# Gated DeltaNet on one core: another order of the input products in three stretches, and later starts for the eight recurrences

## The chip, the cores and the metric

The kernel runs on one core of a Trainium2 chip. The metric is the device time of one execution in microseconds (us); lower is better. The engines are named as the profile names them: PE is TensorE's matmul (PEld its weight load), DVE is VectorE, ACT is ScalarE, POOL is GpSimd, and SP is SyncE, which issues nearly all DMAs. Each engine works through its own instructions strictly in the order of the program and waits on semaphores for the others.

## The reference, cut to what matters

The whole program is one inference step of a two-layer trunk: a gated DeltaNet layer, then an RWKV-7 layer, over 1,104 token rows (64 sample rows, 16 meta tokens, 1,024 prompt rows). The change touches the gated DeltaNet layer alone. Its core, cut from the reference:

```
proj = xn @ w_in                                  # q, k, v and the gate z for all heads
qkv, new_buf = causal_conv(qkv, conv_buf, conv_w) # 4 taps along the tokens, then SiLU
L = jnp.where(strict, jnp.einsum('nbhik,nbhjk->nbhij', kb, k) * decay, 0.0)
A = L + jnp.eye(chunk, dtype=L.dtype)
sol = lax.linalg.triangular_solve(A, rhs, left_side=True, lower=True, unit_diagonal=True)
u, wk = sol[..., :DV], sol[..., DV:]
def step(S, inp):                                 # once a chunk, in order
    v_new = u_c - jnp.einsum('bhck,bhkv->bhcv', w_c, S)
    o = jnp.einsum('bhck,bhkv->bhcv', qd_c, S) + jnp.einsum('bhij,bhjv->bhiv', a_c, v_new)
    S = S * jnp.exp(gl_c)[..., None, None] + jnp.einsum('bhck,bhcv->bhkv', kd_c, v_new)
o = rmsnorm(o, gn_w) * jax.nn.silu(z.reshape(B, T, GDN_V_HEADS, GDN_HEAD_V))
```

There are 16 value heads and 8 query/key heads, so a key head serves a pair of value heads. For each pair: project q, k, two v's and two z's; convolve q, k and v; invert a unit lower triangular matrix for each block of tokens; run the recurrence over the blocks; normalise and gate.

## The kernel before

**Pairs, products, stretches, slots.** The layer is worked in eight pairs of value heads, j = 0 to 7. Each pair needs six products with the resident input: keys `k`, queries `q`, values `v` and `w`, gates `x` and `y`. A product has three token segments (384, 384 and 336 wide), a segment 24 matmuls, issued in two halves of 12. A half with whatever is hung behind it is a **slot**; a product is six slots. The products stand in eight stretches, one string of `ORDER` each: the first has four products (slots -24 to -1), the next six have six (36 slots each), the last has eight. In the stretch of pair j the gates `x`, `y` are those of pair j-1. Slot 0 is the start of the stretch of pair 1, slot 36 that of pair 2, and so on; the products end at slot 264.

**Events.** All other work of PE and ACT in this part is hung on slot numbers by `at(u, f)`: an event with u in [n, n+1) is issued behind the matmuls of slot n. For PE and ACT the order in the program is this order by hand. DVE, POOL and SP take their order from the scheduler of the framework, which merges what the events give.

**What a product hangs on DVE.** The conv of one segment of k, q, v or w is three multiply-adds on DVE (L526, writes `cvy`; the first tap is on ACT), then the SiLU (L532, one instruction, two in the first segment). A gate segment is one DVE instruction (L834, `zg`). A segment of values is then turned by three PE transposes (`f`) and scaled on DVE into `bv` (L825, method `gdn_value_rows`).

**The inverse.** For each pair, scores of the keys (L702 to L712) go through DRAM into the tile `invA`: 72 blocks of 32x32, inverted together on DVE by 31 steps of two instructions (L573 `invtmp`, L575 `invT`), released two or three at a time by the events `inv`. The event `spread` (time `sp`) issues the rest, copies the transpose (L743 `invA`), and sends the inverse through DRAM (`g_t`, `g_u`) into the tiles `T1n` and `TT`. The four `merges` then join the 32-blocks on PE: `y32` (writes `rY`, the first reader of `T1n`), `u32` (`rU`), `y64` and `u64`. They stand 6.5, 4.5, 3.5 and 1.5 slots ahead of the recurrence's start a.

**The recurrence.** It begins at slot a = `first[j]` (one call at a-1, then 26 calls, one a slot). A block of tokens takes three slots: k·S and q·S on PE, X on DVE (L883; L880 and L881 in block 0); TT·X on PE, w on ACT; the new state S (L905) and output o (L916) on DVE. The PE tiles of it are `rA`. The state of block n is read by PE one slot after it is asked for. Norms, gating (`mog` on PE, L1077 on DVE) and stores follow at fixed distances from a.

**What `first` sets.** In `front_events` the score decays, the inverse and others are placed by a0, the start of the recurrence before, as well as by the stretch's own base b; for pairs 3 to 7 the inverse starts at k + 9.3 with k = e + 4.7 and e = a0 - 3.4 as a rule, that is a0 + 10.6.

## Time and profile before

| | |
|---|---|
| Median of 3 runs | 2171.39 us (2170.72 to 2176.32) |
| The profiled execution: time, span | 2173.21 us, 2171.5 us |
| Granted TensorE clock, mean | 0.982 |
| PE busy | 2046.2 us, 94% |
| PEld busy | 1905.8 us, 88% |
| DVE busy | 1583.4 us, 73% |
| ACT busy | 1283.1 us, 59% |
| POOL busy | 834.9 us, 38% |

Slot -24 begins at 39.8 us of the span and the last product ends at 1014.6 us. The starts of the stretches are 105.07, 247.18, 376.52, 496.24, 615.36, 734.30, 853.10 and 972.54 us (slots 0, 36, ... 252). "Idle before" in a row of the timeline is the time that this engine did nothing just before it, with what ended it. A waiting engine holds up everything behind it on its own queue. PE busy includes the pipelined ends of matmuls, so a stretch with PE at 99% has no room that shows as idle.

### The profile page before, as it was taken

What the parts mean: (1) busy time and instruction counts of PE and PEld (TensorE: products, weight loads), DVE (VectorE), ACT (ScalarE), POOL (GpSimd) and SP (SyncE); (2) the same over time, 40 slices, a digit from 0 to 9 for tenths busy, and PEclk for the clock granted to TensorE, in tenths of its full rate; (3) what the DMA queues carried; (4) which work ended last, traced back from release to release, by engine and by line L of the source; (5) the groups of instructions that cost most, each with busy time, mean ns of one, the idle gap of its engine ahead of it and who ended that gap; (6) DMA issues with size and microseconds to landing.
All of it is one profiled execution on the core that took longest, in us unless ns stands there. A gap on an engine that the chain in (4) does not pass through costs nothing. (4 is left out here: it accounts for less than half of the span.)

```text
span 2171.5 us, 54811 instructions
## 1 busy us (share of the span) xinstructions
PE 2046.2 (94%) x20418; PEld 1905.8 (88%) x20418; DVE 1583.4 (73%) x4212; ACT 1283.1 (59%) x3750; POOL 834.9 (38%) x1136
## 2 busy tenths in 40 slices
PE   6969899999999999999999999889899999999997
PEld 5959899999999999998899999889798988888876
DVE  6968879698888979795334676757979557767755
ACT  4536565656565665656533365664747446677774
POOL 3523334334343333334231352344524254444444
PEclk9979999999999999999999999999999999999999
DMA  3424343424333333335345115655555486677754
GB/s 120 122 58 105 77 108 90 118 79 107 90 97 106 106 97 104 97 102 159 106 129 135 63 54 191 220 160 174 169 180 158 117 224 175 188 234 225 228 178 139
DMA packets 430724, 292.52 MB, mean 135 GB/s; under 512 B 147337, under 2 KB 413050, under 8 KB 430458
## 3 DMA queue, kind: packets, MB, share of 16 engines
q1 hardware_dynamic: 430458, 289.02, 46.2%
q8 instruction: 161, 2.64, 0.5%
q14 instruction: 105, 0.86, 0.1%
HBM read 197.55 MB, written 91.37 MB: 133 GB/s over the span
## 5 line engine op out<-in xcount | busy, mean ns | idle before, releaser
L91 POOL TENSOR_TENSOR wlo<-wraw,whi 128x512 fp32r<-128x512 f32 (+1 forms) x246 | 331.1, 1348 | 465.6 <-ACT whi L87 413.9
L77 PE MATMUL d<-xc,whi 128*128 128x384 f32 (+2 forms) x1006 | 279.5, 337 | 4.8 <-ACT whi L87 4.1
L526 DVE SCALAR_TENSOR_TENSOR cvy<-raw,cw,cvy 128x408 f32<-128x408 f32 (+2 forms) x288 | 199.0, 692 | 17.1 <-ACT cvy L63 15.7
L87 ACT CAST whi<-wraw 128x512 fp32r<-128x512 f32 (+1 forms) x246 | 149.8, 611 | 88.1 <-PE d L77 51.2
L77 PEld LDWEIGHTS d<-xc,whi 128*128 128x128 f32 (+1 forms) x1006 | 183.4, 189 | 7.8 <-ACT whi L87 4.8
L77 PE MATMUL d<-xc,wlo 128*128 128x384 f32 (+3 forms) x476 | 157.7, 340 | 2.7 <-POOL wlo L91 2.7
L77 PE MATMUL dz<-xc,whi 128*128 128x384 f32 (+1 forms) x480 | 153.9, 338 | 0.0
L77 PE MATMUL dv<-xc,whi 128*128 128x384 f32 (+1 forms) x480 | 152.4, 337 | 0.0
L77 PE MATMUL d<-xa,whi 128*128 128x384 f32 (+3 forms) x450 | 142.1, 340 | 4.5 <-ACT whi L87 1.7
L63 ACT ACTIVATE o<-rA,gcol 128x128 f32<-128x128 f32 x128 | 42.0, 366 | 116.9 <-DVE S L905 116.7
L573 DVE TENSOR_TENSOR invtmp<-invA,invT 72x31 f32<-72x31 f32 (+15 forms) x248 | 102.2, 412 | 3.2
L77 PE MATMUL dv<-xa,whi 128*128 128x384 f32 (+1 forms) x288 | 99.1, 344 | 0.0
L77 PE MATMUL dz<-xa,whi 128*128 128x384 f32 (+1 forms) x288 | 98.6, 342 | 0.0
L575 DVE TENSOR_TENSOR invT<-invT,invtmp 72x31 f32<-72x31 f32 (+15 forms) x248 | 95.0, 383 | 3.3
L77 PEld LDWEIGHTS d<-xc,wlo 128*128 128x128 f32 (+1 forms) x476 | 89.3, 189 | 6.8 <-POOL wlo L91 3.6
L77 PEld LDWEIGHTS dz<-xc,whi 128*128 128x128 f32 x480 | 89.4, 189 | 4.6 <-issue 4.5
L77 PEld LDWEIGHTS d<-xa,whi 128*128 128x128 f32 (+1 forms) x450 | 83.9, 189 | 8.2 <-issue 3.7
L77 PEld LDWEIGHTS dv<-xc,whi 128*128 128x128 f32 x480 | 89.2, 188 | 1.4 <-issue 1.4
L77 PE MATMUL d<-xa,wlo 128*128 128x384 f32 (+3 forms) x252 | 84.9, 337 | 1.4 <-POOL wlo L91 1.4
L77 PE MATMUL dk<-xc,whi 128*128 128x384 f32 (+1 forms) x240 | 79.3, 349 | 0.0
L77 PE MATMUL dq<-xc,whi 128*128 128x384 f32 (+1 forms) x240 | 77.0, 338 | 0.0
L1335 DVE SCALAR_TENSOR_TENSOR mixs<-xb,pcol,mixs 128x320 f32<-128x320 f32 (+2 forms) x96 | 68.6, 725 | 5.9 <-ACT mixs L63 5.6
(542 smaller groups left out, 6801.0 us busy)
## 6 DMA issues: line engine op xcount, KB each, us to landing
wraw<-in_gdn_w_in SPq DMA_DIRECT2D x96, 256.0 KB
wraw<-in_rwkv_w_rkvz SPq DMA_DIRECT2D x80, 256.0 KB
Sb<-in_state_gdn SPq DMA_DIRECT2D x64, 256.0 KB
sldcak<-cakd SPq DMA_DIRECT2D x24, 576.0 KB
wraw<-in_rwkv_w_o SPq DMA_DIRECT2D x42, 256.0 KB
E<-drow SPq DMA_DIRECT2D x24, 384.0 KB
attn<-drow SPq DMA_DIRECT2D x24, 384.0 KB
wraw<-in_gdn_w_out SPq DMA_DIRECT2D x36, 256.0 KB
```

What stands on the lines that cost most here:

```text
L63: return self.nc.scalar.activation(out, in_, func, bias=bias, scale=scale, **kw)
L77: self.nc.tensor.matmul(out, lhsT, rhs, start=start, stop=stop)
L87: nc.scalar.copy(hi, x)
L91: e.tensor_tensor(lo, x, hi.bitcast(F32), op=ALU.subtract)
L526: nc.vector.scalar_tensor_tensor(y[0][:, 0:wd], raw[:, k:k + wd], cw[k], y[0][:, 0:wd], op0=ALU.mult, op1=ALU.add)
L573: nc.vector.tensor_tensor(tmp, A[:, j, j + 1:32].unsqueeze(2).broadcast_to([nb, n, m]), Tv[:, j, 0:m].unsqueeze(1).broadcast_to([nb, n, m] ...
L575: nc.vector.tensor_tensor(Tv[:, j + 1:32, 0:m], Tv[:, j + 1:32, 0:m], tmp, op=ALU.subtract)
L1335: nc.vector.scalar_tensor_tensor(x[:, f:], xb[:, 8 + a + f:8 + b], mu, x[:, f:], op0=ALU.mult, op1=ALU.add)
```

## The change

Three things, all in where work stands; nothing is computed otherwise.

1. The second stretch (pair 1) goes from `kxyqvw` to `xkyvqw`: gate, keys, gate, values, queries, values. The third and fourth go to `kxyvqw`.
2. The recurrences start later. In slots: 9, 43, 78, 114, 150, 186, 222, 258 before; 14.5, 48.5, 83.5, 118.5, 153.5, 188.5, 224.5, 260.5 now. The gaps between them are 34, 35 and five times 36 before; 34, four times 35 and twice 36 now. Events placed by a or a0 move with them; products don't.
3. The sample states of pairs 3 to 7 are not loaded before a0 + 3.3, and their value rows not before a0 + 5.8 + 9s (two limits that held for earlier pairs only).

```diff
-ORDER = ("kqvw", "kxyqvw", "kxyqvw", "kxyqvw", "kxyqvw", "kxyqvw", "kxyqvw", "kxyqvwXY")
+ORDER = ("kqvw", "xkyvqw", "kxyvqw", "kxyvqw", "kxyqvw", "kxyqvw", "kxyqvw", "kxyqvwXY")
...
-        first = [9, 43] + [base[j + 1] + 6 for j in range(2, 8)]
+        first = [14.5, 48.5, 83.5, 118.5, 153.5] + [base[j + 1] + 8.5 for j in range(5, 8)]
...
-                inv, per, kk, ss, rd = [k + 9.3 + n for n in range(15)], 2, (b + 11.8, qb + 4.2), b + 13.2, (qb + 6.4, qb + 9.9)
+                inv, per, kk, ss, rd = [k + 9.3 + n for n in range(15)], 2, (b + 11.8, qb + 4.2), max(b + 13.2, a0 + 3.3), (qb + 6.4, qb + 9.9)
...
-                u = max(v + 5.4 + 2 * s, a0 + 9 * s + 5.8 + 0.2 * h if 0 < j < 3 else -99)
+                u = max(v + 5.4 + 2 * s, a0 + 9 * s + 5.8 + 0.2 * h if j else -99)
```

On DVE, in the second half of the inverse of pair 0, at the start of the second stretch (slots 0 to 6). Before:

```order
L573 TENSOR_TENSOR invtmp_1117<-invA_921,invT_923 72x255
L526 SCALAR_TENSOR_TENSOR cvy_1461<-raw_1400,cw_404,cvy_1461 128x408
L575 TENSOR_TENSOR invT_923<-invT_923,invtmp_1117 72x17x15
L532 SCALAR_TENSOR_TENSOR vt_1472<-raw_1315,cvy_1381 128x336
L526 SCALAR_TENSOR_TENSOR cvy_1461<-raw_1400,cw_404,cvy_1461 128x408
L573 TENSOR_TENSOR invtmp_1146<-invA_921,invT_923 72x256
L526 SCALAR_TENSOR_TENSOR cvy_1461<-raw_1400,cw_404,cvy_1461 128x408
L809 TENSOR_SCALAR qeps_1003<-qeps_1003 128x9
L575 TENSOR_TENSOR invT_923<-invT_923,invtmp_1146 72x16x16
```

Now, at the same place:

```order
L573 TENSOR_TENSOR invtmp_1117<-invA_921,invT_923 72x255
L834 SCALAR_TENSOR_TENSOR zg_1442<-zg_1442,dz_1399 128x384
L532 SCALAR_TENSOR_TENSOR vt_1451<-raw_1315,cvy_1381 128x336
L575 TENSOR_TENSOR invT_923<-invT_923,invtmp_1117 72x17x15
L573 TENSOR_TENSOR invtmp_1146<-invA_921,invT_923 72x256
L575 TENSOR_TENSOR invT_923<-invT_923,invtmp_1146 72x16x16
L573 TENSOR_TENSOR invtmp_1149<-invA_921,invT_923 72x255
L809 TENSOR_SCALAR qeps_1003<-qeps_1003 128x9
L575 TENSOR_TENSOR invT_923<-invT_923,invtmp_1149 72x15x17
L573 TENSOR_TENSOR invtmp_1152<-invA_921,invT_923 72x252
L825 TENSOR_TENSOR bv_1296<-f_1494,sk_542 128x3x128
```

A gate segment (L834) stands where three conv instructions of the keys stood; two more L834 and, five steps ahead of the end, three L526 of the keys follow further down.

On DVE, at the start of the inverse of pair 3, behind the state of block 3 (from 0) of the recurrence of pair 2, which stands behind slot 88 before and behind slot 93 now. Before:

```order
L905 SCALAR_TENSOR_TENSOR S_5203<-S_5203,eglb_136,rA_5634 128x128
L573 TENSOR_TENSOR invtmp_5717<-invA_5566,invT_5568 72x31
L575 TENSOR_TENSOR invT_5568<-invT_5568,invtmp_5717 72x31
L916 TENSOR_TENSOR o_5628<-o_5628,rA_5633 128x128
L573 TENSOR_TENSOR invtmp_5720<-invA_5566,invT_5568 72x60
L916 TENSOR_TENSOR o_5628<-o_5628,rA_5634 128x128
L575 TENSOR_TENSOR invT_5568<-invT_5568,invtmp_5720 72x30x2
L883 SCALAR_TENSOR_TENSOR X_5741<-rA_5745,gcol_135,bv_4674 128x128
L883 SCALAR_TENSOR_TENSOR X_5742<-rA_5746,gcol_135,bv_4674 128x128
L573 TENSOR_TENSOR invtmp_5761<-invA_5566,invT_5568 72x87
```

Now:

```order
L905 SCALAR_TENSOR_TENSOR S_5297<-S_5297,eglb_136,rA_5725 128x128
L573 TENSOR_TENSOR invtmp_5828<-invA_5651,invT_5653 72x31
L526 SCALAR_TENSOR_TENSOR cvy_5785<-raw_5741,cw_404,cvy_5785 128x384
L575 TENSOR_TENSOR invT_5653<-invT_5653,invtmp_5828 72x31
L916 TENSOR_TENSOR o_5719<-o_5719,rA_5724 128x128
L916 TENSOR_TENSOR o_5719<-o_5719,rA_5725 128x128
L526 SCALAR_TENSOR_TENSOR cvy_5785<-raw_5741,cw_404,cvy_5785 128x384
L573 TENSOR_TENSOR invtmp_5831<-invA_5651,invT_5653 72x60
L532 SCALAR_TENSOR_TENSOR vt_5801<-raw_5662,cvy_5713 128x64
L532 SCALAR_TENSOR_TENSOR vt_5801<-raw_5662,cvy_5713 128x320
L526 SCALAR_TENSOR_TENSOR cvy_5785<-raw_5741,cw_404,cvy_5785 128x384
```

The inverse began beside gate products, with no conv between its first steps; now it begins beside the values, and conv and SiLU instructions stand between them from the first step on.

## The prediction

> **What bounds the kernel now.** First the page's busy shares and slices:

> ```profile
> PE 2046.2 (94%) x20418; PEld 1905.8 (88%) x20418; DVE 1583.4 (73%) x4212; ACT 1283.1 (59%) x3750; POOL 834.9 (38%) x1136
> PE   6969899999999999999999999889899999999997
> DVE  6968879698888979795334676757979557767755
> PEclk9979999999999999999999999999999999999999
> ```

> PE has no free time in most slices; slice 3 shows a hole, there alone with a lowered clock. So the change is worth what it does to PE's waits. Second, PE's waits over the layer:

> ```profile
> PE rY L77 <- DMA T1n<-g_t: 28.2, 6, 20.0
> PE rA L77 <- DVE o L916: 5.8, 11, 0.8
> PE rA L77 <- DVE S L905: 2.2, 6, 0.7
> ```

> One wait counts: `y32` (tile `rY`), the first merge, for the inverse. Third, the timeline of PE, where it falls (pairs 0, 1 and 2; the last row is pair 3, and pairs 3 to 7 have none):

> ```profile
> 133.43 0.31 PE L77 MATMUL rY<-T1n,E 32*32 32x32 f32 x2 [20.05 <-DMA T1n<-g_t]
> 134.32 1.86 PE L77 MATMUL rY<-T1n,E 32*32 32x32 f32 x62 [0.59 <-DMA T1n<-g_t]
> ...
> 255.50 0.31 PE L77 MATMUL rY<-T1n,E 32*32 32x32 f32 x2 [5.98 <-DMA T1n<-g_t]
> 256.18 2.13 PE L77 MATMUL rY<-T1n,E 32*32 32x32 f32 x70 [0.37 <-DMA T1n<-g_t]
> ...
> 374.32 0.22 PE L77 MATMUL rY<-T1n,E 32*32 32x32 f32 x2 [0.51 <-DMA T1n<-g_t]
> 375.27 1.32 PE L77 MATMUL rY<-T1n,E 32*32 32x32 f32 x70 [0.73 <-DMA T1n<-g_t]
> ...
> 494.99 1.33 PE L77 MATMUL rY<-T1n,E 32*32 32x32 f32 x72
> ```

> The DMA is only the messenger. Fourth, SyncE's rows of pair 0, and windows from the first inverse step to the end of L743 (pair 0's second half, then pairs 1, 2, 3):

> ```profile
> 128.18 0.27 SPq L746 DMA_DIRECT2D g_t<-invT  x1
> 131.03 1.40 SPq L749 DMA_DIRECT2D T1n<-g_t  x3
> ...
> 112.50:129.20 16.70, 0.88 (x7) 0.61 (x5) 15.63 (x41) 1.41 (x7) 2.45 (x1) 0.65 0.09 25
> 195.00:249.50 54.50, 52.97 (x408) 51.13 (x406) 53.84 (x149) 35.38 (x121) 17.39 (x28) 1.00 0.27 78
> 318.70:369.30 50.60, 49.52 (x386) 48.30 (x385) 48.23 (x140) 31.45 (x107) 16.23 (x26) 1.00 0.26 78
> 437.40:489.50 52.10, 50.98 (x390) 49.26 (x389) 49.53 (x139) 32.77 (x112) 15.58 (x26) 1.00 0.29 82
> ```

> `g_t` leaves when the last step ends (128.18), PE starts 5.3 us later. DVE (third pair of figures) is busy 53.84 of 54.5 us in pair 1 and 49.53 of 52.1 in pair 3: during an inverse DVE is full, and it sets when `y32` may run. In pair 3 L743 ends at 489.5, and PE comes to `rY` 5.5 us later (494.99) without waiting, about what the DMAs take in pair 1 (249.5 to 255.5): that pair has next to no slack.

> **The change, part by part.** Prices on DVE over the layer (mean ns behind the bar), and a bare slot, the half product at 156.09:

> ```profile
> L526 DVE SCALAR_TENSOR_TENSOR cvy<-raw,cw,cvy 128x408 f32<-128x408 f32 (+2 forms) x288 | 199.0, 692 | 17.1 <-ACT cvy L63 15.7
> L905 DVE SCALAR_TENSOR_TENSOR S<-S,eglb,rA 128x128 f32<-128x128 f32 x113 | 34.7, 339 | 1.3 <-PE rA L77 1.1
> L916 DVE TENSOR_TENSOR o<-o,rA 128x128 f32<-128x128 f32 x112 | 29.4, 278 | 2.3 <-ACT o L63 2.1
> L532 DVE SCALAR_TENSOR_TENSOR vt<-raw,cvy 128x64 f32<-128x64 f32 (+1 forms) x64 | 26.7, 435 | 4.9 <-ACT raw L63 4.8
> L825 DVE TENSOR_TENSOR bv<-f,sk 128x384 f32<-128x384 f32 x48 | 26.3, 549 | 17.8 <-PE f L74 17.7
> L834 DVE SCALAR_TENSOR_TENSOR zg<-zg,dz 128x384 f32<-128x384 f32 (+1 forms) x47 | 25.1, 534 | 25.7 <-ACT zg L63 25.7
> L1077 DVE SCALAR_TENSOR_TENSOR zg<-mog,hgn,zg 128x384 f32<-128x384 f32 (+1 forms) x42 | 24.9, 593 | 0.5
> L881 DVE TENSOR_SCALAR X<-bv 64x128 f32<-64x128 f32 x16 | 8.6, 538 | 0.2
> L880 DVE SCALAR_TENSOR_TENSOR X<-sS,gcol,bv 64x128 f32<-64x128 f32 x16 | 5.4, 340 | 0.1
> ...
> 156.09:158.28 2.19, 2.19 (x14) 2.19 (x15) 0.51 (x1) 2.17 (x7) 0.21 (x1) 1.00 0.00 0
> ```

> *Pair 0.* `y32` moves from behind slot 2 to behind slot 8. Six slots come ahead of it, two of them 336 wide (2.19 x 336/384 = 1.9): 4 x 2.19 + 2 x 1.9 = 12.6 us, and three value transposes, under 0.5 us. PE arrived at 133.43 - 20.05 = 113.4 and now arrives at 126.4. DVE loses three L526 and gains three further down, so these cancel, and gains three L834 (1.6 us) and one L825 (0.5): data at 133.4 + 2.1 = 135.5. The waits of 20.6 us become 9.1 + 0.6 = 9.8: **-10.8 us**. Bounds: -13 if DVE fits the new rows into its gaps (16.7 - 15.63 = 1.1 us in its window), -8 if POOL, silent in the stall (2.45 us busy), slows DVE as it works on.

> *Pairs 1 to 7.* What does the later start do to an inverse? Its first step stands behind the state of block 3 of the recurrence before, so it moves with a0, while the products stay. In pairs 3 to 7 it used to start beside gate products, which give DVE one instruction a segment; now it starts beside products with a conv, four to six a segment. By the program's order, between the first L573 and L743 stand (conv rows L526, all rows): pair 1 24 and 147 before, pairs 3 to 7 19 and 137; now pairs 1 to 7: 21/141, 24/154, 27/158, 24/154, 27/156, 24/147, 24/143. The slots of PE from that start to `y32`: 17, 18 and five times 19 before; 18, four times 19 and twice 20 now. These rows can't be shortened and PE can't pass them, so I scale from pair 1 of before, which was as full: 24 conv rows, 17 slots, and PE waited 5.98 + 0.37 = 6.3 us. Each slot more gives DVE 2.2 us, since the recurrence in it is the same length; each row more costs its price:

> - Pair 1: -3 L526, -1 L532, -2 L905, -2 L916, -1 L1077, +1 L825, +1 each of L880, L881: -3.0. One slot: 6.3 - 3.0 - 2.2 = 1.1. Against 6.3: **-5.2**.
> - Pair 2: +3 L825 and the two X rows, +2.5; two slots: 6.3 + 2.5 - 4.4 = 4.4. Against 1.2: **+3.2**.
> - Pair 3: +3 L526, +2 L532, +2 L825, two X, +5.0: **+6.9**. Pair 4: +1 L532, +2 L825, two X, +2.4: **+4.3**. Pair 5: +3 L526, +1 L532, +1 L825, two X, +3.9: **+5.8**. All against no wait at `rY`.
> - Pairs 6, 7: no more rows and three slots more, 6.3 - 6.6: **0**.

> The same rule on the kernel before gives pair 2 about 0 (it was 1.2) and pairs 3 to 7 none (true), so it errs by some 1.5 us a pair, and alike in all. Where the wait appears is open: part may fall at `rA` (state late), the rest at `rY`.

> *The clock* after waits:

> ```profile
> 133.40:141.30 7.90, 7.28 (x88) 6.99 (x89) 2.18 (x7) 0.59 (x2) 0.14 (x1) 0.50 0.28 43
> 255.50:260.90 5.40, 5.03 (x81) 4.83 (x82) 2.43 (x7) 0.00 (x0) 0.00 (x0) 0.51 0.27 42
> 376.90:380.30 3.40, 3.40 (x14) 3.29 (x12) 3.11 (x9) 2.68 (x9) 0.00 (x0) 0.50 0.29 42
> ```

> Half clock for 7.9, 5.4 and 3.4 us costs about half of each: 3.9, 2.7 and 1.7. I take 1.7 for each new wait and 3.3 for pair 0: -0.6, -1.0, 0, then 3 x 1.7 = 5.1: **+3.5** (0 to +10). [...]

> *The end.* The last recurrence moves 2.5 slots past the products, into the hand-over to the output projection, where PE has 6 us idle:

> ```profile
> 1014.60:1064.00 49.40, 43.26 (x302) 39.77 (x301) 22.22 (x58) 37.68 (x167) 13.79 (x13) 1.00 0.56 170
> ```

> PE's work is only moved; I take 0 (-2 to +3). The sample states' later load (pairs 3 to 7) isn't waited for by PE in any row; 0.

> **Sum** against the profiled 2173.2: -10.8 - 5.2 + 3.2 + 6.9 + 4.3 + 5.8 + 3.5 = +7.7, 2180.9. The median of the runs lies 1.8 lower, so 2179.

> **The rivals.**

> *Faster: DVE takes the extra rows.* Pairs 2 to 5, if from first step to L743 DVE needs no more than some 52 us there. Then only pairs 0 and 1 count: -10.8 - 5.2 - 1.6 (clock) = 2154. For: DVE idles 2.6 us in pair 3's window, and 27% of the whole span. Against: pair 1's 53.84 of 54.5.

> *Even.* The waits come, but 2 us smaller each, without half clock: 7.7 - 8 - 5.1 = -5: 2166.

> *Slower still: conv rows get dearer in full windows.*

> ```profile
> 195.00:249.50 54.50, 16.74 (x24) 1.00 0.27 78
> 437.40:489.50 52.10, 11.41 (x19) 1.00 0.29 82
> ```

> L526 took 0.70 us in the full window and 0.60 in the other. Another 0.1 on 24 to 27 rows is 2.6 us a pair, 10 in four, and a second half-clock spell each, 7: 2196. [...]

> *The change doesn't reach pair 0:* the scheduler's rows delay its inverse as much as PE gains; its wait stays near 20: 2190.

> **How the numbers follow.** Forecast (+2 to +14) 0.44; DVE takes the rows 0.20; even 0.17; dearer rows 0.14; pair 0 unchanged 0.05. A change under 0.3% (6.5 us) can't be told from none. Slower: 0.7 of the forecast, 0.31, and 0.19 for the last two: 0.50. Same: 0.13 of the forecast and 0.14 of even: 0.27. Faster: 0.20 and 0.03 of even: 0.23. The range leaves out half of the fastest case and the ends of the slow ones: 2157 to 2194; the forecast's own is 2173 to 2186.

> **What would show it.** In the new profile: `rY` of pair 0 waiting 8 to 12 us, pair 1 under 3; in pairs 2 to 5 DVE over 95% busy from first L573 to L743 for 55 us or more, with PE waits of 4 to 7 us at `rY` or `rA` and a spell of half clock behind. Wrong if those windows stay near 52 us, or if pairs 6 and 7 wait as well.

## The result, and the profile after

| | Before | After |
|---|---|---|
| Median of the runs | 2173.86 us (2170.72 to 2183.70, 4 runs) | 2208.71 us (2204.24 to 2211.79, 4 runs) |
| Profiled execution: time, span | 2173.21, 2171.5 us | 2211.79, 2210.1 us |
| Mean granted TensorE clock | 0.982 | 0.974 |
| Products of pairs 1 to 7 (slot 0 to 264) | 909.5 us | 937.5 us |
| From there to the end | 1156.9 us | 1166.9 us |

The ratio is 1.0156, with a 95% interval of 1.0131 to 1.0181: 35 us slower. The direction was forecast, the size was not: 2179 us was predicted, and 2208.7 lies outside the range of 2157 to 2194.

The page of the profile after (PE's busy time, and the granted clock in 40 slices):

```profile
PE 2067.2 (94%) x20418; PEld 1920.8 (87%) x20418; DVE 1561.3 (71%) x4212; ACT 1291.0 (58%) x3750; POOL 839.1 (38%) x1136
PEclk9989999999999999999999999989999999999999
```

PE does the same 20418 instructions and takes 21 us longer over them, DVE 22 us less: the time went into waits of PE and into slow matmuls behind them. PE's waits in the products (us in total, times, longest), after:

```profile
PE rY L77 <- DMA T1n<-g_t: 28.4, 12, 10.8
PE rA L77 <- DVE S L905: 6.2, 8, 1.6
PE rA L77 <- DVE o L916: 5.8, 15, 0.8
PE flast L74 <- POOL last L516: 5.0, 3, 2.3
PE rA L77 <- ACT w L63: 3.9, 3, 1.9
PE mhist L74 <- ACT ktok L63: 2.7, 1, 2.7
PE f L74 <- DVE vt L532: 2.4, 4, 1.0
PE fsr L77 <- POOL raw L508: 1.7, 1, 1.7
```

The first row is the one that the prediction summed, and it has not moved: 28.2 us before, 28.4 now, in 12 waits instead of 6. What is new stands below it. Four of these rows (`flast`, `w`, `ktok`, `raw`) do not occur before, and in them PE waits for ScalarE or GpSimd, not directly for a vector row.

Added up from the trace between slot 0 and slot 264. Waits are idle times of PE over 0.05 us. Half clock is the time that PE worked at half clock, times the share not granted; what PE idled at half clock is in the waits already. PE at work is the rest.

| us | y32 (`rY`) | other waits of PE | half clock | PE at work | sum |
|---|---|---|---|---|---|
| Before | 28.2 | 13.7 | 7.8 | 859.8 | 909.5 |
| After | 28.4 | 30.9 | 21.2 | 857.1 | 937.5 |
| Forecast of the difference | +4.2 | 0 | +3.5 | 0 | +7.7 |
| Measured difference | +0.2 | +17.2 | +13.4 | -2.7 | +28.0 |

Behind the products another 10.0 us differ. From the last product to the first matmul of the tile `dlora`, which belongs to the second layer, it took 244.2 us instead of 238.5: 1.8 us more of waits, 1.0 more of half clock, and 2.8 more of PE's work, which is what left the products with the last recurrence. So from slot 0 to the second layer the change costs 33.7 of the 35 us: 19.2 of waits (0.2 of them at `y32`), 14.4 of half clock, and 0.1 of PE at work. That stretch behind the products took 237.2 to 241.9 us in the nine kernels of this study whose last recurrence starts at slot 258, and 239.5 to 248.2 us in the eleven where it starts at 260.5. The second layer itself took 913.4 to 930.3 us (918.4 before, 922.7 after), with no order by the starts, and is not followed further.

The waits at `y32`, the first and, where there is one, a second row of pairs 0 to 5 in PE's timeline after:

```profile
137.20 0.28 PE L77 MATMUL rY<-T1n,E 32*32 32x32 f32 x2 [10.83 <-DMA T1n<-g_t]
...
262.00 0.22 PE L77 MATMUL rY<-T1n,E 32*32 32x32 f32 x2 [1.40 <-DMA T1n<-g_t]
...
385.89 0.24 PE L77 MATMUL rY<-T1n,E 32*32 32x32 f32 x2 [3.43 <-DMA T1n<-g_t]
...
513.45 0.31 PE L77 MATMUL rY<-T1n,E 32*32 32x32 f32 x2 [6.19 <-DMA T1n<-g_t]
514.31 0.42 PE L77 MATMUL rY<-T1n,E 32*32 32x32 f32 x7 [0.55 <-DMA T1n<-g_t]
...
638.48 0.24 PE L77 MATMUL rY<-T1n,E 32*32 32x32 f32 x2 [1.97 <-DMA T1n<-g_t]
...
762.93 0.24 PE L77 MATMUL rY<-T1n,E 32*32 32x32 f32 x2 [1.61 <-DMA T1n<-g_t]
```

And the inverse windows from the first L573 to the end of L743 (length, then PE, PEld, DVE, ACT and POOL busy, clock, DMA), pairs 1 to 6 after:

```profile
200.40:254.60 54.20, 50.63 (x387) 49.12 (x387) 51.89 (x143) 32.93 (x107) 15.94 (x27) 0.97 0.23 66
323.90:381.00 57.10, 55.07 (x417) 52.55 (x418) 55.22 (x156) 36.26 (x119) 19.17 (x30) 1.00 0.24 72
447.30:508.30 61.00, 57.19 (x430) 54.42 (x428) 58.06 (x160) 36.76 (x119) 22.44 (x33) 1.00 0.25 73
576.20:634.30 58.10, 54.70 (x417) 52.17 (x418) 53.47 (x156) 37.66 (x124) 21.05 (x31) 1.00 0.25 74
698.70:758.70 60.00, 54.90 (x418) 52.52 (x417) 57.24 (x157) 36.06 (x120) 20.21 (x31) 1.00 0.26 75
822.20:877.70 55.50, 53.40 (x412) 51.44 (x411) 53.45 (x149) 35.84 (x122) 16.58 (x28) 1.00 0.26 76
```

This half came as forecast: the windows of pairs 2 to 5 grew from 51 or 52 to 57 to 61 us with DVE 92% (pair 4) to 97% busy, where over 95% was forecast, and pair 6 has no wait at `y32`.

### The profile page after: what moved, and what is told of

It is laid out like the page before. It is cut to its first block, busy times and chain, and to the rows that moved or that the text cites. A ratio compares the mean times of both kernels' runs of the same rounds, so it can differ in the third digit from the quotient of the medians.

```text
span 2210.1 us, 54843 instructions
## 1 busy us (share of the span) xinstructions
PE 2067.2 (94%) x20418; PEld 1920.8 (87%) x20418; DVE 1561.3 (71%) x4212; ACT 1291.0 (58%) x3750; POOL 839.1 (38%) x1136
## 5 line engine op out<-in xcount | busy, mean ns | idle before, releaser
L77 PE MATMUL d<-xc,whi 128*128 128x384 f32 (+2 forms) x1006 | 278.4, 336 | 0.6 <-DVE xc L309 0.6
L526 DVE SCALAR_TENSOR_TENSOR cvy<-raw,cw,cvy 128x408 f32<-128x408 f32 (+2 forms) x288 | 185.3, 644 | 20.8 <-ACT cvy L63 19.2
L77 PEld LDWEIGHTS d<-xc,whi 128*128 128x128 f32 (+1 forms) x1006 | 183.3, 189 | 3.2 <-DVE xc L309 1.0
L77 PE MATMUL d<-xc,wlo 128*128 128x384 f32 (+3 forms) x476 | 157.3, 339 | 2.2 <-POOL wlo L91 2.2
L77 PE MATMUL dz<-xc,whi 128*128 128x384 f32 (+1 forms) x480 | 156.6, 344 | 0.0
L77 PE MATMUL dv<-xc,whi 128*128 128x384 f32 (+1 forms) x480 | 154.8, 341 | 0.0
L77 PE MATMUL d<-xa,whi 128*128 128x384 f32 (+3 forms) x450 | 142.2, 340 | 7.4 <-ACT ev L2354 4.2
L63 ACT ACTIVATE o<-rA,gcol 128x128 f32<-128x128 f32 x128 | 42.0, 369 | 117.3 <-DVE S L905 116.8
L77 PE MATMUL dz<-xa,whi 128*128 128x384 f32 (+1 forms) x288 | 100.5, 349 | 0.0
L77 PE MATMUL dv<-xa,whi 128*128 128x384 f32 (+1 forms) x288 | 99.7, 346 | 0.0
L77 PEld LDWEIGHTS dz<-xc,whi 128*128 128x128 f32 x480 | 91.5, 193 | 4.8 <-issue 4.5
L573 DVE TENSOR_TENSOR invtmp<-invA,invT 72x31 f32<-72x31 f32 (+15 forms) x248 | 93.5, 377 | 2.5
L77 PEld LDWEIGHTS d<-xa,whi 128*128 128x128 f32 (+1 forms) x450 | 84.2, 190 | 12.0 <-ACT ev L2354 4.5
L77 PEld LDWEIGHTS d<-xc,wlo 128*128 128x128 f32 (+1 forms) x476 | 89.3, 189 | 6.2 <-POOL wlo L91 3.2
L77 PEld LDWEIGHTS dv<-xc,whi 128*128 128x128 f32 x480 | 90.7, 191 | 0.2 <-issue 0.2
L77 PE MATMUL d<-xa,wlo 128*128 128x384 f32 (+3 forms) x252 | 84.8, 337 | 1.3 <-POOL wlo L91 1.1
L77 PE MATMUL dk<-xc,whi 128*128 128x384 f32 (+1 forms) x240 | 79.5, 353 | 0.0
L77 PE MATMUL dq<-xc,whi 128*128 128x384 f32 (+1 forms) x240 | 76.9, 338 | 0.0
```

The source lines that it names most:

```text
L63: return self.nc.scalar.activation(out, in_, func, bias=bias, scale=scale, **kw)
L77: self.nc.tensor.matmul(out, lhsT, rhs, start=start, stop=stop)
L526: nc.vector.scalar_tensor_tensor(y[0][:, 0:wd], raw[:, k:k + wd], cw[k], y[0][:, 0:wd], op0=ALU.mult, op1=ALU.add)
L573: nc.vector.tensor_tensor(tmp, A[:, j, j + 1:32].unsqueeze(2).broadcast_to([nb, n, m]), Tv[:, j, 0:m].unsqueeze(1).broadcast_to([nb, n, m] ...
```

## The experiments

"Products" is slot 0 to 264 of the profiled execution, and the next four columns are its parts as above; "to `dlora`" is from there to the second layer. Each run was compared with the kernel before on the same chip, whose median there was 2173.4 to 2178.5 us. The profiled execution is one of several and need not be like the median: for steady and taps_before it was the fastest (2184.0 and 2133.3 us), for after, after_both, taps_after and taps_after_both the slowest (2211.8, 2203.4, 2161.9 and 2153.6 us).

| Run | Median, us | Ratio to before (95%) | Products | y32 | other waits | half clock | at work | to `dlora` |
|---|---|---|---|---|---|---|---|---|
| before | 2173.9 | 1 | 909.5 | 28.2 | 13.7 | 7.8 | 859.8 | 238.5 |
| after | 2208.7 | 1.0156 (1.0131 to 1.0181) | 937.5 | 28.4 | 30.9 | 21.2 | 857.1 | 244.2 |
| steady | 2189.6 | 1.0073 (1.0048 to 1.0098) | 915.1 | 27.6 | 24.7 | 5.7 | 857.1 | 239.5 |
| light | 2213.7 | 1.0172 (1.0133 to 1.0210) | 935.8 | 24.8 | 30.9 | 22.9 | 857.2 | 244.2 |
| order_only | 2198.8 | 1.0101 (1.0072 to 1.0130) | 935.4 | 39.7 | 20.2 | 17.5 | 857.9 | 237.7 |
| order_pair1 | 2209.1 | 1.0158 (1.0122 to 1.0194) | 935.3 | 27.3 | 28.8 | 23.3 | 855.8 | 246.6 |
| last_later | 2203.3 | 1.0116 (1.0086 to 1.0147) | 928.9 | 24.8 | 26.9 | 20.6 | 856.7 | 248.2 |
| steady_scale | 2190.7 | 1.0072 (1.0048 to 1.0095) | 922.9 | 23.4 | 29.9 | 14.2 | 855.5 | 246.5 |
| steady_both | 2189.3 | 1.0059 (1.0038 to 1.0079) | 915.1 | 28.4 | 20.7 | 9.5 | 856.4 | 242.5 |
| after_both | 2197.7 | 1.0111 (1.0085 to 1.0138) | 932.9 | 32.1 | 22.4 | 21.6 | 856.9 | 243.3 |
| taps_before | 2140.1 | 0.9841 (0.9809 to 0.9872) | 875.5 | 17.6 | 4.7 | 2.5 | 850.8 | 237.2 |
| taps_after | 2156.7 | 0.9920 (0.9892 to 0.9948) | 894.9 | 9.7 | 22.0 | 8.6 | 854.7 | 244.7 |
| taps_after_both | 2150.1 | 0.9867 (0.9849 to 0.9885) | 879.5 | 9.7 | 13.9 | 2.4 | 853.5 | 246.3 |
| taps_steady_both | 2151.1 | 0.9882 (0.9863 to 0.9901) | 885.0 | 17.5 | 10.0 | 3.9 | 853.5 | 240.9 |
| starts105 | 2180.8 | 1.0032 (1.0012 to 1.0051) | 914.6 | 24.7 | 20.5 | 8.5 | 860.9 | 241.2 |
| starts12 | 2197.9 | 1.0100 (1.0060 to 1.0140) | 933.4 | 29.2 | 29.6 | 15.1 | 859.6 | 241.9 |
| back12 | 2201.5 | 1.0116 (1.0094 to 1.0137) | 932.4 | 19.7 | 36.1 | 17.3 | 859.4 | 238.9 |
| back34 | 2182.9 | 1.0038 (1.0025 to 1.0052) | 917.5 | 14.8 | 30.0 | 10.9 | 861.9 | 238.0 |
| back34_both | 2195.7 | 1.0096 (1.0060 to 1.0132) | 932.7 | 26.5 | 27.0 | 19.1 | 860.1 | 237.3 |
| pair1_back34 | 2190.3 | 1.0072 (1.0050 to 1.0095) | 930.0 | 28.5 | 24.6 | 15.8 | 861.2 | 237.5 |

**The late start alone (steady).** The kernel before, in its own order, and

```diff
-        first = [9, 43] + [base[j + 1] + 6 for j in range(2, 8)]
+        first = [9, 43] + [base[j + 1] + 8.5 for j in range(2, 8)]
```

> The kernel before, in its own order of products, with only the recurrences of pairs 2 to 7 put 8.5 slots into a stretch (pairs 0 and 1 stay at 9 and 43). Two theories of the 28.6 us that the change loses up to the end of the products. Backlog: vector rows pile up in the inverse windows of pairs 2 to 5 (57 to 61 us instead of 51 to 52), everything queued behind them on VectorE comes late, and PE waits for whatever that is. Here the windows of pairs 3 to 7 have 24 conv rows and 20 slots, as pairs 6 and 7 of the change, so no wait at y32 from pair 3 on, and at most +4 us against the kernel before: 2172 to 2178. Offset: 8.5 slots itself puts the recurrence's norm and scores in front of the last tokens, the history and the state columns at a stretch's border; pairs 6 and 7 of the change lost 2.1 us a stretch and 2.8 at the end without any wait at y32, so six stretches and the end give +14 to +18: 2188 to 2192.

15 us slower than before by the medians, the time of the theory that was called "offset", though the windows of pairs 3 to 7 brought no more than 0.9 us at `y32`. The profiled execution was 10.8 us slower. In it five stretches and the end lost 9 us (0.3, 1.3, 2.8, 1.4, 2.1 and 1.2), where that theory had 14 to 18. PE's waits from slot 108 on, without a wait at `y32` worth the name:

```profile
PE rA L77 <- ACT w L63: 6.9, 4, 1.9
PE flast L74 <- POOL last L516: 5.2, 5, 2.3
```

Both are waits behind something else in a queue. GpSimd at the last stretch border of this run:

```profile
976.32 0.99 POOL L653 TENSOR_SCALAR_AFFINE_SELECT attn<-attn 128x768 f32<-128x768 f32 x1 [5.42 <-DMA attn<-drow]
977.28 1.29 POOL L91 TENSOR_TENSOR wlo<-wraw,whi 128x512 fp32r<-128x512 f32 x1
979.77 1.33 POOL L103 TENSOR_TENSOR ors<-ovar,cvals 128x6 f32<-128x6 f32 x1 [1.20 <-DVE ovar L1059]
981.05 0.57 POOL L516 COPY last<-raw 128x3 f32<-128x3 f32 x1
```

The 0.57 us copy of the last tokens, for which PE waits, stands behind the norm's root (`ors`), and that waits for DVE; 8.5 slots into a stretch the norm falls on the border. And ScalarE, where the recurrence's `w` starts 3.5 us after PE has ended the matmuls that it reads (956.6 by PE's timeline):

```profile
954.60 0.70 ACT L63 ACTIVATE o<-o,ors 128x128 f32<-128x128 f32 x2 [0.27 <-DVE ors L113]
...
957.55 0.70 ACT L63 ACTIVATE o<-o,ors 128x128 f32<-128x128 f32 x2
...
959.54 0.57 ACT L63 ACTIVATE cvy<-raw,cw 128x336 f32<-128x336 f32 x1
960.02 0.61 ACT L63 ACTIVATE w<-rA,nbp 128x128 f32<-128x128 f32 x2
```

In the run after, the scaling stands ahead of `ktok` in the same way, and PE's `mhist` waited 2.7 us for that at 236.78:

```profile
234.76 0.69 ACT L63 ACTIVATE o<-o,ors 128x128 f32<-128x128 f32 x2 [2.06 <-DVE ors L113]
235.36 0.73 ACT L1103 COPY sS<-fsr 64x256 f32<-64x256 f32 x2
236.10 0.62 ACT L63 ACTIVATE ktok<-mktok,gcol 128x128 f32<-128x128 f32 x2
```

**Lighter windows (light).** The starts of the change, and from pair 2 on a gate product inside each window:

```diff
-ORDER = ("kqvw", "xkyvqw", "kxyvqw", "kxyvqw", "kxyqvw", "kxyqvw", "kxyqvw", "kxyqvwXY")
+ORDER = ("kqvw", "xkyvqw", "kxvyqw", "kxvyqw", "kxvyqw", "kxqyvw", "kxqyvw", "kxqyvwXY")
```

> The changed kernel with the same starts of all recurrences, but from pair 2 on the products in an order that puts a gate product inside the inverse window (kxvyqw in pairs 2 to 4, kxqyvw in 5 to 7): 15 to 21 conv rows from first step to copy instead of 24 to 27. Backlog: waits at y32 shrink to 0 to 1.5 us each from pair 2 on, the other waits and the half-clock spells behind them go too, the gains of pairs 0 and 1 (10.8 and 5.2 us forecast, 9.3 and 4.7 measured at y32) stay: 2153 to 2168. Offset: the norm and the last tokens still meet at the border, 2 to 3 us a stretch: 2172 to 2185. Uneven spacing (35 slots instead of 36 squeezes the recurrence itself): no better than the changed kernel less the waits at y32, about 2190.

All three theories missed: 2213.7. Pair 2 lost its wait as the rows say, but pairs 3 and 5 waited 4.9 and 4.4 us in windows of 60.5 and 62.1 us in which DVE idled 5.3 and 8.7 us. In these windows DVE waited for PE (2.8 us for `f`, 1.5 for `rA` in pair 5), and the inverse behind it with it. So the price of a row gave the wait only where DVE was full.

**Fewer conv rows (taps_after, taps_before).** The conv's last tap is left out in both, a third of all L526:

```diff
-            for k in range(1, 4):
+            for k in range(1, 3):
```

> The changed kernel with one of the three vector rows (L526) of each conv segment left out, so the conv lacks its last tap: 96 rows of 0.6 us less on VectorE, 8 or 9 of them (5 us) in each inverse window. Backlog: windows fall from 55 to 61 us to 50 to 56, nearly all new waits of pairs 2 to 5 vanish, and the kernel ends at 2155 to 2175. Offset: it keeps 2 to 3 us a stretch and stays above the kernel before with the same tap left out by 5 us or more.

> The kernel before with the same vector row left out. It has waits only in pairs 0 (20.6 us) and 1 (6.3): pair 1's wait and its half clock go, pair 0's inverse has 5 conv rows less behind it and shortens by 2 to 4 us. Backlog: 2158 to 2167, and the changed kernel with the tap left out is 0 to 10 us faster than this one. Offset: the changed kernel stays slower than this one.

The change ended where "backlog" put it; the kernel before did not, it gained 35 us where at most 17 was expected, since its other waits fell too (13.7 to 4.7 us). The difference between the two fell from 35 to 16.6 us and did not go. Of the terms, `y32` in pairs 2 to 5 all but went, and the half clock, 13.4 us more than before with all taps, is 6.1 more (8.6 against 2.5). The other waits stayed, 22.0 against 4.7, which is +17.3 and as much as with all taps. So over half of the new half clock came with the full windows, and the other waits did not. They are, in the run after without the tap:

```profile
PE rY L77 <- DMA T1n<-g_t: 9.6, 5, 8.3
PE rA L77 <- ACT w L63: 5.1, 4, 2.5
PE flast L74 <- POOL last L516: 4.6, 2, 2.3
```

**The queues (last_later, steady_scale, steady_both, after_both).** What waits is moved: the last tokens' transposition two slots on, and the norm's scaling (`o` by `ors`) two and a half slots on, behind `w`. The first alone in the change; the second alone and both in steady; both in the change.

```diff
-        at(max(qb, vb) + 6.95, lambda: self.last_tokens(j, g().H))
+        at(max(qb, vb) + (8.95 if j else 6.95), lambda: self.last_tokens(j, g().H))
...
-                at(9 * s + 10.2 + 0.5 * tt, lambda s=s, tt=tt: nm[s](tt))
+                at(9 * s + (12.7 if s < 2 else 10.2) + 0.5 * tt, lambda s=s, tt=tt: nm[s](tt))
```

> The changed kernel with the transposition of the last tokens (flast on TensorE) two slots later from pair 1 on. On GpSimd the copy that it needs (L516) now stands behind the norm's square root, which waits for VectorE, which is behind with its rows; PE waited 5.0 us for it at three stretch borders (1.9, 0.7, 2.3). If that is a wait of its own, taken out by moving what waits, PE comes through the borders and the kernel is 4 to 8 us faster than the changed one (a half-clock spell of 1.7 us goes too): 2200 to 2205. If PE is only held by VectorE's backlog, the wait turns up at the next instruction that needs a vector row, and the time stays at 2206 to 2212.

> The run with the starts 8.5 slots into a stretch from pair 2 on and the order of before (2189.6 us, 15 more than before), with the scaling of the norm (o by ors on ScalarE, blocks 0 to 5) two and a half slots later, so that it stands behind the next step's w and not ahead of it. Theory queues: PE's wait for w at slot 30 of each stretch (1.6 to 1.9 us, five times) and for ktok go, 8 to 10 us less: 2179 to 2182. Theory rows: VectorE is late itself and PE waits for its rows S, X or o instead: 2186 to 2191.

> The same, and the transposition of the last tokens two slots later, so that it waits for no GpSimd row behind the norm's root (0.7 us at four borders and 2.3 at the last). Theory queues: all that the late start costs without a wait at y32 is in these two, and the time is back at that of before: 2173 to 2179. Theory rows: 2182 to 2188.

> The changed kernel with both. The later transposition alone gave 2203.3 instead of 2208.7. Theory queues: the waits for w (3.9 us) and for ktok (2.7 us and a half-clock spell of 1.7) go too: 2194 to 2200. Theory rows: those waits turn up at the vector rows that are late in the full windows: 2201 to 2206.

In the change the first gave 5.4 us and both 11.0 (2208.7 to 2203.3 and 2197.7), inside the ranges of the theory of the queues. The ratios to before on the same chip are 1.0156, 1.0116 and 1.0111, and the products took 937.5, 928.9 and 932.9 us, so a gain of the second edit on top of the first is not shown. What the traces do show is whose waits these were: `flast`, `w` and `ktok`, 11.6 us in the change, come to 0.1 in after_both, whose longest are

```profile
PE rY L77 <- DMA T1n<-g_t: 32.0, 14, 10.8
PE rA L77 <- DVE o L916: 8.3, 17, 0.9
PE rA L77 <- DVE S L905: 4.8, 7, 1.4
PE rA L77 <- DVE X L883: 1.8, 2, 0.9
```

The other waits together fell by less, from 30.9 to 22.4, because PE then waited more for DVE; `y32` took 3.7 us back, and the products came to only 4.6 us less. In steady they gave nothing (2190.7 and 2189.3 after 2189.6), as the theory of the rows says. With the scaling alone moved, the waits for `w` were gone and those at `flast` were 2.2 to 2.9 us at five borders; with both moved, PE waited as long for DVE (from slot 108 on, steady_both):

```profile
PE rY L77 <- DMA T1n<-g_t: 5.2, 8, 0.8
PE rA L77 <- DVE X L883: 3.5, 4, 0.9
PE f L74 <- DVE invT L575: 3.4, 5, 0.7
PE rA L77 <- DVE o L916: 3.1, 4, 0.8
```

There the windows have 24 conv rows and 20 slots, and the summed price of their rows left 0.3 us to spare: take one wait away, and DVE is next in line.

**Both at once (taps_after_both, taps_steady_both).** The two edits above with the tap left out.

> The changed kernel with the conv's last tap left out (L526 twice instead of three times a segment) and, as in after_both, the norm's scaling of blocks 0 to 5 two and a half slots later and the last tokens' transposition two slots later. With the tap left out alone: 2156.7, the kernel before with the tap left out 2140.1. Theory two limits side by side: with the rows gone and the queues cleared, the waits for w (5.1 us), the last tokens (4.6), ktok (2.3) and a half-clock spell or two go: 2140 to 2147, of the 16.6 us at most 7 left. Theory something else (the order, the 35 slots): 2150 to 2158.

> The starts 8.5 slots into a stretch from pair 2 on and the order of before, the conv's last tap left out and both queue waits taken away. With all taps this was 2189.3, 16 us over before. Theory two limits: level with the kernel before without the tap, 2136 to 2145. Theory something else: the late start keeps costing 8 to 16 us, 2148 to 2156.

By the number alone, 2150.1 us lies in the second theory's range. But the kernel before ran 3.8 us slower on this chip than on that of taps_after, and measured against it the change is now 0.26% above the kernel before without the tap (0.9867 against 0.9841, intervals that overlap) instead of 0.79%. The products take 879.5 us against 875.5, not 894.9. So rows and queues together carry most of it, 15.4 of 19.4 us in the products: 8.1 of other waits, 6.1 of half clock, 1.2 of PE at work. Behind the products 9.1 us remain up to `dlora` in these two profiles, 6.0 of them half clock. The starts of steady stay 0.41% over before and their products 9.5 us, where level was expected; 5.3 of that are other waits, and 2.7 are PE at work, which was not found. The kernel before was not run with the two queue edits; its own trace has none of the waits that they take away.

**The order (order_only, order_pair1).** The kernel before with the changed order and its own starts; and the change with the old order in pairs 2 and 3.

```diff
-ORDER = ("kqvw", "xkyvqw", "kxyvqw", "kxyvqw", "kxyqvw", "kxyqvw", "kxyqvw", "kxyqvwXY")
+ORDER = ("kqvw", "xkyvqw", "kxyqvw", "kxyqvw", "kxyqvw", "kxyqvw", "kxyqvw", "kxyqvwXY")
```

> The kernel before with the changed order of products in pairs 1, 2 and 3, all recurrences starting where they did. If the order itself costs (other buffers, other neighbours on each engine), it shows here: 2184 or more. If only the starts cost, pair 1 alone changes: its window has 26 conv rows and 16 slots, so its wait at y32 goes from 6.3 to about 11 us, the rest stays: 2176 to 2181.

> The changed kernel with all its starts, but the order of products of pairs 2 and 3 put back to kxyqvw; only pair 1 keeps xkyvqw. The order alone, with the starts of before, cost 26 us up to the end of the products: 2.3, 9.6, 8.1 and 6.0 us in the stretches of pairs 1 to 4. Theory order: values ahead of queries in pairs 2 and 3 cost by themselves (the third query norm lands in the next stretch behind decay rows, and weights and state loads meet the DMAs of y32), whatever the starts; then this run is 8 to 14 us faster than the change: 2194 to 2200. Theory starts: with the late starts the two orders are equal (the windows have the same 24, 27, 24, 27 conv rows), and the loss of the change comes from where the recurrence falls: 2203 to 2212.

With early starts the order alone costs 24 us; with late starts the order of pairs 2 and 3 makes no difference (2209.1 and 2208.7). The two halves of the change do not add up. Pair 1 waited 10.2 us for its 26 rows in 16 slots (11.1 by the price), but pairs 2 and 3 waited 4.9 and 5.2 where the rows gave 0.7 and none. In pair 3 the window was 2.8 us longer than before (54.9 against 52.1). SyncE shows a possible reason for more, pair 3 of order_only:

```profile
505.80 0.30 SPq L746 DMA_DIRECT2D g_t<-invT  x1
506.19 0.38 SPq L428 DMA_DIRECT2D wraw<-in_gdn_w_in  x1
506.96 0.49 SPq L745 DMA_DIRECT2D g_u<-invA  x1
507.54 0.38 SPq L1090 DMA_DIRECT2D Sb<-in_state_gdn  x1
509.00 1.63 SPq L749 DMA_DIRECT2D T1n<-g_t  x3
```

A load of weights and one of sample states, 256 KB each, went out between the inverse's two transfers. PE's first `rY` came at 513.9, 3.3 us after the last of the three T1n issues; before it came 2.4 us after them without waiting at all, at 494.99. From the end of L743 to `rY` it was 7.0 us instead of 5.4, so the loads can account for some 1.6 of the 5.2 us. That they are the cause is argued, not tried.

**Smaller and shorter shifts (starts105, starts12, back12, back34, pair1_back34, back34_both).** Starts 10.5, 44.5, 79 or 12, 46, 80, 114 and then 6 slots into a stretch, in the old order, with part 3 of the change; 12, 46, 80, 114 with `xkvyqw` in pair 1 and `kxvyqw` in 2 to 4; and the change's first two starts with 34 slots between until pair 5 is back at 6:

```diff
-        first = [14.5, 48.5, 83.5, 118.5, 153.5] + [base[j + 1] + 8.5 for j in range(5, 8)]
+        first = [14.5, 48.5, 82.5, 116.5, 150.5] + [base[j + 1] + 6 for j in range(5, 8)]
```

with `kxvyqw` in pairs 2 to 4 (back34, and back34_both with the two queue edits) or with only pair 1 reordered (pair1_back34).

> The same with a small shift: 10.5, 44.5, 79, then 6 slots into a stretch from pair 3 on; order of before. y32 of pair 0 stands behind five slots instead of three, its wait falls from 20.6 to about 17 to 19 us (three conv rows more ahead of the copy); pair 1's from 6.3 to 3.7. Theory order: 2166 to 2173. Theory starts: one and a half slots already bring the recurrence among other rows: 2175 to 2185.

> The kernel before with its own order of products in all pairs, and only the starts moved: 12, 46, 80, 114, then 6 slots into a stretch from pair 4 on. Theory order: without a new order hardly anything is lost; pair 0's y32 waits 15 us instead of 20.6, pair 1's 1 to 3 instead of 6.3, pairs 2 and 3 get waits of 2 to 5 us (21 and 25 conv rows, 17 slots), so 2166 to 2176. Theory starts: each stretch in which the recurrence is moved loses 5 to 8 us as in the run with 12, 46, 80, 114 and the other order: 2185 to 2201.

> A smaller shift: starts 12, 46, 80, 114, then 6 slots into a stretch from pair 4 on; order xkvyqw in pair 1 and kxvyqw in pairs 2 to 4. Pair 0's y32 stands behind six slots instead of nine, so its wait is about 15 us instead of 11.3 (20.6 before), pair 1's is gone (17 conv rows in its window). Offset and backlog both: 5 + 6 us less at y32 and 2 to 4 of clock, pairs 4 to 7 as before: 2160 to 2168. If moved products cost as in the run before: 2172 to 2185.

> Pairs 0 and 1 start as in the change (14.5 and 48.5), then every 34 slots (82.5, 116.5, 150.5) until pair 5 is back at 6 slots into a stretch; pairs 2 to 4 have the order kxvyqw. Windows: 18, 16, 14 and 21 conv rows in pairs 2 to 5. Offset: pairs 5 to 7 and the end cost nothing any more, pairs 2 to 4 cost 1 to 4 us each, and pairs 0 and 1 keep their gain of 14: 2162 to 2174. Backlog alone: nothing is left but the gain: 2153 to 2160. If what was lost with the lighter windows of the run before (PE and VectorE waiting for each other in turn wherever a product is moved away from its tuned place) is what counts, it is slower than before: 2178 to 2195.

> Starts 14.5, 48.5, 82.5, 116.5, 150.5, then 6 slots into a stretch; order xkyvqw in pair 1 alone, all other pairs as before. Windows of pairs 2 to 4: 24 conv rows in 18 slots (kxvyqw had 18, 16 and 14, and came to 2182.9). Theory order: fewer moved products outweigh the fuller windows, 2170 to 2180. Theory backlog, which goes by the rows of the windows: 7, 7 and 4 us at y32 and the half clock behind, 2190 to 2200.

> Starts 14.5, 48.5, 82.5, 116.5, 150.5 and then 6, order kxvyqw in pairs 2 to 4 (2182.9), with both. Theory queues: the waits for ktok (2.7 and 1.7 of clock) and for w go: 2174 to 2179, level with before. Theory rows: 2180 to 2185.

None beats the kernel before. The nearest are 1.0032 (starts105) and 1.0038 (back34). starts105, starts12, back34 and pair1_back34 came out in the slowest of their ranges; back12 missed both of its by 16 us or more. They show what the gain in pair 0 needs: with start 12 its `y32` still waited 19.4 us in the old order, where three products of conv rows follow (22 L526 ahead of the copy), and 15.3 us with the gate first (13). back34 has the least wait at `y32` with all taps (14.8 us), and loses it to 30.0 us of other waits, 12.7 of them for `o`, to 3.0 us more of half clock and 2.1 of PE at work. back34_both was expected 4 to 9 us faster than back34 and was 13 slower: edits that helped in one arrangement did harm in the next.

The starts of the change with the whole order of before were not run, nor was part 3 of the change by itself, so what each of the three parts costs alone stays open.

## Why the prediction was right or wrong

**Pairs 0 to 7 at `y32`: right in mechanism, in size but for pairs 4 and 5.** Measured 11.3, 1.6, 3.8, 6.7, 2.6, 2.3, 0, 0; forecast 9.8, 1.1, 4.4, 6.9, 4.3, 5.8, 0, 0. Scaling from the full window of pair 1 (rows at their price, 2.2 us a slot) held within 1.5 us in six pairs. What pairs 4 and 5 lack stands mostly at `rA`, as the prediction left open: in their windows PE waited 2.3 and 2.2 us for the state S, where it was 0.3 in each before, and in pair 5 the 1.9 us at `flast` stand two slots ahead of `y32`. The term at `y32` is 4.0 short (+0.2 instead of +4.2), and the waits for S in all are 4.0 more (2.2 to 6.2). In the runs that keep the order, the same scaling gave 6.3 against 6.0 and -0.3 against 0 to 0.9 (steady), and 9.3 against 9.8 (starts12, pair 3; worked out afterwards, the expectation on record had 2 to 5). It failed where DVE idles in the window (light) and perhaps where transfers collide (order_only).

**Waits of PE elsewhere, put at nothing: the step that failed.** "Where the wait appears is open: part may fall at `rA` (state late), the rest at `rY`", says the prediction, and its sum has no term for any other place. The other waits grew by 17.2 us, 13 of them not foreseen. The working followed VectorE's queue and asked of the inverse alone who waits for it. It did not ask what stands behind what on ScalarE and GpSimd once the recurrence meets other products: the norm's scaling ahead of `w` and of `ktok`, the norm's root ahead of the last tokens. That these rows come from the two queues is shown by moving what waits: they went from 11.6 to 0.1 us in the change and from 12.0 to 0.5 without the tap. What that saved in waits is 8.5 and 8.1 us, because part of it turned up at DVE. Beside them 4.0 us are the state, 1.7 `fsr` and 1.0 `f`, which were not followed; the 2.8 us that PE waited at `mog` before are gone, and the rest is in rows under 0.7 us.

**Pairs 6 and 7, and the end, at 0: wrong in the same way.** There was no wait at `y32`, but 2.0 us in the stretch of slot 216 and 2.8 us from slot 252 to the end of the products; the prediction had named waits in pairs 6 and 7 as what would show it wrong. Behind the products 5.7 us more passed up to the second layer, where the bounds of the end were -2 to +3; 2.8 of these are work that was only moved, as the prediction says.

**The clock at +3.5: the other term that was mis-sized, by 9.9.** Measured is +13.4 in the products, above the upper bound of +10. The prediction charged 1.7 us to each new wait at `y32`. The spells come in pieces of 3.41 us, each worth those 1.7 where PE works through it; pairs 2 and 4 had two and pair 3 three, not one, so pairs 2 to 5 cost 9.6 us more where 5.1 was forecast. Another 4.9 us come from spells behind other waits, at 192.0, 236.4 and 1004.4 us. Pairs 0 and 1 saved 1.1 (1.6 forecast). The reading that slice 3 alone has a lowered clock rests on digits in which 9 is 90% or more: a piece of 3.41 us in a slice of 54 us does not show there.

**The rivals.** "DVE takes the extra rows" and "even" fell: pairs 2 to 5 did wait and the clock did fall. "Conv rows get dearer" fell too, though its time (2196) was the nearest. L526 in the seven stretches together, before and after:

```profile
sum 867.00, DVE 172.72; mean DVE 24.67
```

```profile
sum 893.00, DVE 159.71; mean DVE 22.82
```

For the same 254 rows DVE needed less, not more. In the products every L526 without a GpSimd row beside it took 0.55 to 0.65 us, in both traces; those over 1 us, 16 before (up to 4.13) and nine after (up to 1.61), all ran beside one. In the longest window, that of pair 3, L526 took 0.62 us, where this rival needed more than the 0.70 of pair 1 before:

```profile
447.30:508.30 61.00, 16.68 (x27) 1.00 0.25 73
```

"The change doesn't reach pair 0" fell with 11.3 us.

## What to carry to other kernels

When a chain is moved against other work, list for every engine on its way which instruction of the chain now stands behind which foreign one, and what that one waits for; a full queue is only the first place to look. Waits at one place are not a sum of causes: here vector rows and two short in-order queues held PE side by side, and taking away one moved part of the wait to the other, or all of it. And where the engine that bounds the kernel has no slack, a shift that gains once is paid for in each of the stretches that it reaches, by small waits and the half clock behind them (17.2 and 13.4 us more here): count the stretches first.

## What the runs showed of the hardware

```profile
185.18:188.60 3.42, 3.42 (x27) 3.42 (x26) 3.26 (x10) 2.14 (x7) 3.17 (x2) 1.00 0.65 177
188.60:192.01 3.41, 1.54 (x9) 0.88 (x7) 3.41 (x14) 1.25 (x5) 0.20 (x2) 1.00 0.36 79
192.01:195.42 3.41, 3.41 (x14) 3.41 (x15) 1.97 (x9) 1.53 (x7) 1.16 (x2) 0.50 0.62 197
```

Waits of 0.7, 0.5 and 0.7 us left PE 45% of one piece busy behind a full one, and the next piece ran at half clock, with 14 matmuls in it where its neighbours have 25 to 27. Each spell in the products of the change began behind a piece that was idle for 47 to 100%, and no piece idle for 45% or less began one there; but before, a piece idle for 36%, by pair 2's waits of 0.51 and 0.73 us, did (373.44 to 376.86), so there is no sharp bound by this measure. So a wait of a given length cost a piece or none here: the 1.9 us behind 188.60 brought one, and the wait of 1.92 us for `w` that ended at 981.87 us, of which 1.4 us fell into one piece, brought none.
